# A streaming softmax on one core: row tiles of 3, 5, 15, 15, 25, 25, 10, 15, 15 instead of 3, 5 and eight times 15

## The chip, the core and the metric

The kernel runs on one core of a Trainium2 chip. The metric is device time in microseconds (us); the median of five runs of the kernel before is 159.82 us (159.80 to 167.6, four of the five between 159.80 and 159.89).

## What is computed

A softmax with temperature 2 over the last axis of a 16 x 1024 x 512 array in 32-bit floats. That is 16,384 rows of 512 numbers, 33.55 MB in and as much out.

```
x_scaled = x / 2.0
exp_x = exp(x_scaled - max(x_scaled, axis=-1))
out = exp_x / sum(exp_x, axis=-1)
```

The kernel takes the exponential without subtracting the row's maximum, and checks afterwards that every row sum lies between 1.0 and 1e30. Only if one does not is everything computed again, with the maximum subtracted (the loops inside `rounds`, L142 to L151). For the inputs here that second way is not taken.

## The kernel before, in words

**Layout.** The 16,384 rows are spread over 128 partitions, so that each partition handles 128 rows. In this text a "row" is from here on one such slot: 128 rows of the input, one on each partition, 2048 bytes on each partition. The 128 rows are cut into tiles by the list `TILES` (L10 to L12): pairs of a row count and a place in `arena`, an on-chip buffer with room for 98 rows (L15). A tile of r rows is moved by one DMA in which each partition gets one contiguous run of r x 2048 bytes: 30,720 bytes for 15 rows. With 128 partitions over 16 DMA engines each engine gets 8 such runs of every tile.

**Loads.** Tile 0 is loaded from SP's queue and all other tiles up to the arena's end from ACT's queue, one behind the other, at the very start (`early`, L153; `loads`, L157; `load`, L113). The two last tiles do not fit and are written over tiles 0 to 2 and tile 3, which must have been stored by then. `LATE` (L14) says which stores each of them waits for, and GpSimd (POOL) issues them: it first waits until the rows below `TURN` (L22) have had their exponential (L176), then for the stores (L178), then issues the load (L179).

**Exponential.** When a tile has landed, TensorE's queue, which has hardly any other work, gives ACT one permit for each chunk of the tile (L193, L194); a chunk is 5 rows (3 for the first tile). So a tile's first exponential can start only when all of the tile has landed. ACT takes the exponential of each row in place and its sum along with it (L204, and the loop `exponentials`, L259 to L276).

**Scaling.** DVE takes groups of up to three chunks of one tile (`pairs`, L82 to L88; in the last tile each chunk alone): a reciprocal of the sums (L166), and one multiplication over the whole group (L169).

**Stores.** SP stores the tiles in order, each when all groups of the tile have been scaled (`store`, L135 to L137; `upto`, L89; L211). Load and store of one tile thus have the same run length.

**End.** After the last exponential POOL, DVE and TensorE check the row sums (L180 to L190), and SP waits for all stores.

A tile's order is therefore: load, exponentials, multiplications, store; the four parts of different tiles run beside each other, and what ties them is the arena's room and the order in three DMA queues: q10 in the profile is ACT's (loads), q1 is SP's (tile 0's load and all stores), q0 is POOL's (the two late loads).

Of the kernel before, what the change touches and what calls it, by code (L numbers as in the profile page):

```python
# [7 lines left out]


TILES = [  # L10
    (3, 0), (5, 3), (15, 8), (15, 23), (15, 38), (15, 53), (15, 68), (15, 83), (15, 0), (15, 15),
]  # L12

LATE = {8: (0, 1, 2), 9: (3,)}  # L14
ARENA = 98  # L15

HEAD = [3]
# [1 line left out]

SPREAD = 1  # L20

TURN = 83  # L22

LO, HI = 1.0, 1.0e30
G = 64
# [3 lines left out]
def kernel(  # L29
# [61 lines left out]
    ld = [nc.alloc_semaphore(f"ld{t}") for t in range(len(tiles))]  # L91
    s_home = {t: nc.alloc_semaphore(f"s_home{t}") for t in LATE}
    s_near = nc.alloc_semaphore("s_near")
# [19 lines left out]
    def load(eng, t):  # L113
        r = tiles[t][1]
        parts = [(0, P, 0, r)]
        if t == SPREAD:
            parts = [(0, P, 0, r - 1), (0, 126, r - 1, r), (126, P, r - 1, r)]
        for p, q, lo, hi in parts:
            eng.dma_start(  # L119
                out=sb(t)[p:q, lo:hi], in_=dram(xf, t)[p:q, lo:hi]  # L120
            ).then_inc(ld[t], 16)

    stored_by = {u: s_home[t] for t, us in LATE.items() for u in us}
    for t, (_, r, at) in enumerate(tiles):
        over = {u for u, (_, ru, au) in enumerate(tiles[:t]) if at < au + ru and au < at + r}
        assert over <= {u for v, us in LATE.items() if v <= t for u in us}

    def landings(ts):
        return 16 * len(list(ts))
# [27 lines left out]
    def loads():  # L157
        for t in range(2, min(LATE)):
            load(nc.scalar, t)

    def program():
# [13 lines left out]
        nc.gpsimd.memset(ones[:, :], 1.0).then_inc(s_ones, 1)  # L175
        nc.gpsimd.wait_ge(s_exp, starts.index(TURN))  # L176
        for t, us in LATE.items():
            nc.gpsimd.wait_ge(s_home[t], landings(us))  # L178
# [143 lines left out]
```

## Time and profile before

| | |
|---|---|
| median of 5 runs | 159.82 us |
| the profiled execution's own time | 159.85 us |
| its span, first to last instruction | 158.5 us |
| time outside the span | 1.35 us |
| bytes read / written | 33.55 / 33.55 MB |
| ACT busy | 80.6 us (51%) |
| DVE busy | 73.2 us (46%) |
| stores: issues, KB each for 15 rows | 10, 3840 |

Times in the profile are counted from the first instruction. A packet in the profile's DMA rows is one contiguous run of one partition, or a 4-byte packet that reports an engine's part of a DMA as done. The share of a queue is the time that its packets took, divided by the time of all 16 DMA engines. A DMA's landing is the moment at which all of its parts are reported.

### The profile page before, as it was taken

How to read it: one execution, taken by the hardware profiler on the slowest of the kernel's cores; microseconds unless marked ns; L12 is line 12 of the kernel's file. 1: busy time of each engine (PE TensorE's matmuls, PEld its weight loads, DVE VectorE, ACT ScalarE, POOL GpSimd, SP SyncE). 2: the span in 40 equal slices, each digit the busy share in tenths (PEclk: the TensorE clock that was granted, in tenths of full speed). 3: DMA queues.
4: the chain of work that ended last, by engine and by line, in shares of the span. 5: the costliest groups of instructions: out<-in, count | busy, mean ns of one | idle time of the engine just before them, and what ended most of it. 6: DMA issues, size and time to landing. Idle time of an engine off the chain costs nothing. (4 is left out here: it accounts for less than half of the span.)

```text
span 158.5 us, 657 instructions
## 1 busy us (share of the span) xinstructions
PE 0.2 (0%) x2; PEld 0.1 (0%) x2; DVE 73.2 (46%) x27; ACT 80.6 (51%) x257; POOL 2.2 (1%) x8
## 2 busy tenths in 40 slices
PE   0000000000000000000000000000000000000000
PEld 0000000000000000000000000000000000000000
DVE  0047001992981990059500991008931990993000
ACT  0590598697498008940399001991498008950000
POOL 0000000000000000000000300000000000010000
DMA  7999998999999999999999999999989898989896
GB/s 267 387 496 395 462 408 349 478 390 481 419 442 426 426 442 426 442 419 450 419 450 419 450 403 465 395 473 395 473 380 488 380 488 380 488 372 496 372 481 264
DMA packets 3025, 67.11 MB, mean 423 GB/s; under 512 B 337, under 2 KB 337, under 8 KB 721
## 3 DMA queue, kind: packets, MB, share of 16 engines
q1 hardware_dynamic: 1584, 34.34, 50.6%
q10 hardware_dynamic: 1152, 24.90, 37.0%
q0 software_dynamic: 288, 7.86, 11.6%
q14 instruction: 1, 0.00, 0.0%
HBM read 33.55 MB, written 33.55 MB: 423 GB/s over the span
## 5 line engine op out<-in xcount | busy, mean ns | idle before, releaser
L271 ACT ACTIVATE arena<-arena x125 | 76.6, 614 | 54.3 <-ACTq L140 54.3
L169 DVE TENSOR_TENSOR arena<-arena,recip 128x7680 f32<-128x7680 f32 (+2 forms) x12 | 70.2, 5847 | 0.4
L166 DVE RECIPROCAL recip<-stats 128x15 f32<-128x15 f32 (+2 forms) x12 | 2.7, 224 | 70.5 <-ACT arena L271 61.5
L271 ACT ACTIVATION_READ_ACCUMULATOR arena<-arena x125 | 23.3, 187 | 0.0
L200 ACT ACT_TABLE_LOAD x1 | 1.3, 1283 | 5.8 <-issue 5.8
L119 POOL DMA_DIRECT2D arena<-in_x_dram x2 | 1.3, 636 | 84.9 <-ACT arena L271 84.9
L204 ACT ACTIVATE arena<-arena 128x512 f32<-128x512 f32 x3 | 1.9, 618 | 0.0
L180 POOL TENSOR_SCALAR inside<-stats 128x128 f32<-128x128 f32 x1 | 0.6, 630 | 51.9 <-ACT arena L271 51.9
L204 ACT ACTIVATION_READ_ACCUMULATOR arena<-arena 128x1 f32 x3 | 0.6, 186 | 0.0
L196 PE MATMUL total<-ones,count 128*1 128x1 f32 x2 | 0.2, 164 | 144.1 <-DVE inside L184 144.1
L184 DVE SCALAR_TENSOR_TENSOR inside<-inside,stats 128x128 f32<-128x128 f32 x1 | 0.3, 285 | 0.0
L188 DVE TENSOR_SCALAR flag<-total 1x1 int32<-1x1 f32 x1 | 0.1, 147 | 0.3 <-PE total L196 0.3
L196 PEld LDWEIGHTS total<-ones,count 128*1 128x1 f32 x2 | 0.1, 80 | 144.1 <-DVE inside L184 144.1
L175 POOL MEMSET ones<- 128x1 f32 x1 | 0.1, 98 | 2.2 <-POOLq L37 2.2
L306 POOL MEMSET const-float32-0.0<- 128x1 f32 x1 | 0.1, 104 | 0.2 <-issue 0.2
L306 POOL MEMSET const-bfloat16-1.0<- 128x1 bf16 x1 | 0.1, 107 | 0.0
L306 POOL MEMSET const-uint8-127<- 128x1 uint8 x1 | 0.1, 107 | 0.0
L306 POOL MEMSET const-float32-1.0<- 128x1 f32 x1 | 0.1, 104 | 0.0
L184 DVE DVE_READ_ACCUMULATOR inside<-inside,stats 128x1 f32 x1 | 0.1, 83 | 0.0
## 6 DMA issues: line engine op xcount, KB each, us to landing
out_dram<-arena SPq DMA_DIRECT2D x8, 3840.0 KB, 26.2
arena<-in_x_dram ACTq DMA_DIRECT2D x6, 3840.0 KB, 46.6
arena<-in_x_dram POOLq DMA_DIRECT2D x2, 3840.0 KB, 33.9
out_dram<-arena SPq DMA_DIRECT2D x1, 1280.0 KB, 23.6
arena<-in_x_dram ACTq DMA_DIRECT2D x1, 1024.0 KB
arena<-in_x_dram SPq DMA_DIRECT2D x1, 768.0 KB, 5.6
out_dram<-arena SPq DMA_DIRECT2D x1, 768.0 KB, 15.5
arena<-in_x_dram ACTq DMA_DIRECT2D x1, 252.0 KB
```

What stands on the lines that cost most here:

```text
L119: eng.dma_start(out=sb(t)[p:q, lo:hi], in_=dram(xf, t)[p:q, lo:hi]).then_inc(ld[t], 16)
L166: nc.vector.reciprocal(out=recip[:, b : b + c], in_=stats[:, b : b + c])._wait_ge(s_exp, ks[-1] + 1).then_inc(s_rec, 1)
L169: nc.vector.tensor_mul(out=arena[:, a : a + c], in0=arena[:, a : a + c], in1=recip[:, b : b + c].unsqueeze(2).to_broadcast([P, c, D]),)._w ...
L175: nc.gpsimd.memset(ones[:, :], 1.0).then_inc(s_ones, 1)
L180: nc.gpsimd.tensor_scalar(out=inside[:, :], in0=stats[:, :], scalar1=LO, scalar2=HI, op0=Alu.max, op1=Alu.min,)._wait_ge(s_exp, len(sizes) ...
L184: nc.vector.scalar_tensor_tensor(out=inside[:, :], in0=inside[:, :], scalar=1.0, in1=stats[:, :], op0=Alu.mult, op1=Alu.is_equal, accum_ou ...
L188: nc.vector.tensor_scalar(out=flag[:, :], in0=total[:, :], scalar1=float(N), scalar2=None, op0=Alu.is_ge,)._wait_ge(s_tot, 1).then_inc(s_f ...
L196: nc.tensor.matmul(total[:, :], lhsT=count[:, :], rhs=ones[:, :], start=True, stop=True)._wait_ge(s_cnt, 2).then_inc(s_tot, 1)
L200: nc.scalar.preload_act_table(Exp)
L204: ins = nc.scalar.activation(out=arena[:, b], in_=arena[:, b], func=Exp, scale=0.5, accum_out=stats[:, b : b + 1],)
L271: ins = nc.scalar.activation(out=data, in_=data, func=Exp, scale=0.5, accum_out=stats[:, r : n_rows - E + 1 + r][:, bass.ds(now, 1)],)
L306: nc = _bacc.Bacc("TRN2", target_bir_lowering=False, num_devices=1)
```

## The change

Only three constants change. The 60 rows of tiles 4 to 7 (four tiles of 15) become three tiles of 25, 25 and 10 rows, so there are nine tiles instead of ten. The two late tiles keep their size, their places and the stores that they wait for, and are now numbers 7 and 8. POOL's first wait is for the exponentials of rows 0 to 62 (up to the end of the first 25-row tile) instead of rows 0 to 82.

```
 TILES = [
-    (3, 0), (5, 3), (15, 8), (15, 23), (15, 38), (15, 53), (15, 68), (15, 83), (15, 0), (15, 15),
+    (3, 0), (5, 3), (15, 8), (15, 23), (25, 38), (25, 63), (10, 88), (15, 0), (15, 15),
 ]
 
-LATE = {8: (0, 1, 2), 9: (3,)}
+LATE = {7: (0, 1, 2), 8: (3,)}
...
-TURN = 83
+TURN = 63
```

What follows from it in the code: a run is 51,200 bytes in the 25-row tiles and 20,480 in the 10-row tile. A 25-row tile gets five permits at once when it has landed; DVE scales it in a group of three chunks and a group of two; its store waits for both. ACT still runs 26 chunks; the DVE groups are 13 instead of 12: of 3 and 5 rows, then 15, 15, 15 and 10, 15 and 10, 10, 15, and three times 5.

## Prediction

> **What bounds the kernel now.** I read the page first, for the engines and the DMA row.
>
> ```profile
> span 158.5 us, 657 instructions
> ...
> PE 0.2 (0%) x2; PEld 0.1 (0%) x2; DVE 73.2 (46%) x27; ACT 80.6 (51%) x257; POOL 2.2 (1%) x8
> ...
> DMA  7999998999999999999999999999989898989896
> ...
> DVE 6%; PE 0%; issue 0%; ACT 0%
> ```
>
> No compute engine is busy for much over half of the span, while the DMA row stands at 8 or 9 in every slice but the first and last. The last line is the chain of work that ended last. It covers 6% only: it begins at 134.43 us with an exponential and ends at 144.3 us, because it doesn't follow transfers. What bounds must be looked for in the queues, so I asked for the DMA view of the stretch from 1 to 158 us (queue: packets, MB, share of 16 engines):
>
> ```profile
> DMA packets 3024, 67.11 MB, mean 427 GB/s; under 512 B 336, under 2 KB 336, under 8 KB 720
> ...
> q1 hardware_dynamic: 1584, 34.34, 51.1%
> q10 hardware_dynamic: 1152, 24.90, 37.4%
> q0 software_dynamic: 288, 7.86, 11.7%
> ```
>
> The shares add up to 100.2%: all 16 DMA engines work without a pause from 1 to 158 us (a little over 100%, since packets overlap slightly). The time is the work of the DMA engines plus 1 us ahead and 0.5 us behind. So a change helps only if it makes that work less, and hurts only if it makes it more or leaves the queues empty for a while. Two things are then wanted: what a packet costs by its size, and how near the queues come to running empty.
>
> For the first I took the stretch from 28.8 to 36.5 us, in which q1 moves only 10,240-byte packets (tile 1's store) and q10 only 30,720-byte ones:
>
> ```profile
> DMA packets 161, 3.31 MB, mean 430 GB/s; under 512 B 0, under 2 KB 0, under 8 KB 0
> ...
> q10 hardware_dynamic: 81, 2.49, 74.8%
> q1 hardware_dynamic: 80, 0.82, 25.0%
> ```
>
> A packet of 30,720 bytes takes 0.748 x 7.7 us x 16 / 81 = 1.138 us, one of 10,240 bytes 0.250 x 7.7 x 16 / 80 = 0.385 us. The line through both is 0.0087 us plus 0.03675 us per 1000 bytes. The packet counts show a second thing: 81 against 80. An engine takes one packet from each queue in turn, whatever its size.
>
> For the second I took the stretches at the end (us, then busy time and instructions of PE, PEld, DVE, ACT, POOL, then clock, DMA share, GB/s):
>
> ```profile
> 131.10:143.80 12.70, 0.00 (x0) 0.00 (x0) 9.04 (x7) 9.29 (x30) 0.63 (x1) 1.00 0.99 428
> 143.80:149.40 5.60, 0.19 (x2) 0.09 (x2) 0.35 (x3) 0.00 (x0) 0.00 (x0) 1.00 1.01 433
> 149.40:158.50 9.10, 0.00 (x0) 0.00 (x0) 0.00 (x0) 0.00 (x0) 0.00 (x0) 1.00 0.88 378
> ```
>
> The last load lands at 131.1 us. Until its tile's store is issued, at 143.83 us, ACT and DVE work 9.3 and 9.0 us, and the DMA engines live on the stores before it (0.99). The store before the last lands at 149.4 us; the last needs the 9.1 us after that.
>
> **The change part by part.**
>
> *Packets.* By the line, a 51,200-byte packet costs 1.890 us and a 20,480-byte one 0.761 us. Each engine loses 4 x 8 packets of 15 rows (load and store: 64 x 1.138 = 72.8 us) and gets 2 x 8 x 2 of 25 rows and 8 x 2 of 10 rows (32 x 1.890 + 16 x 0.761 = 72.7 us): the bytes are the same, and 16 packets' constant part goes, 16 x 0.0087 = 0.14 us, with two 4-byte reports of 0.009 us. As packets overlap a little (the 100.2%), the constant is worth between 0 and that: a gain of 0 to 0.16 us. I take 0.1.
>
> The trace has no 51,200-byte packet. From below it costs its bytes alone, 51.2 x 0.03675 = 1.882 us; from above as much as five packets of 10,240 bytes, 5 x 0.385 = 1.925 us. Over 32 packets on each engine that is 0.3 us less to 1.1 us more than 1.890. I take the line, because it comes out of the nearest row, 30,720 bytes.
>
> *Fixed cost of a DMA.* One load and one store fewer are issued. In the stretch from 132.8 to 147 us q1 works alone, finishes one store and begins the next, with a share of 99.8%: between two DMAs that are both queued there is nothing to save, so I price it at 0. The Trainium skill, "DMA: Bandwidth & Descriptors", section "Anatomy of one DMA — SWDGE (gpsimd) path", fits each DMA as about 2.0 us plus its bytes over 436 GB/s; by that, two DMAs fewer would be an estimated 4 us, and the time about 155.8 us. The 99.8% speaks against it: such a fixed part passes beside the next DMA's bytes here.
>
> *Waits.* A tile's exponentials wait for all of it, and its store for all its groups. I rebuilt the schedule from durations in the trace: an exponential 0.612 us per row (15 rows from 59.85 to 69.03), a multiplication 8.16 us for 15 rows, so 5.4 for 10, a reciprocal 0.28 us, a store's first packet 3.8 us after its issue (35.59 to about 39.3), a POOL load's 5.1 us (87.60 to about 92.7).
> - Until tile 3 has landed (28.8 us) nothing differs.
> - Tile 4: 8 turns on each engine of one load packet (1.890) and one store packet. About 6 packets of tile 1's store are left, then tile 2's store (issued at 35.6) gives two: 6 x 2.275 + 2 x 3.03 = 19.7, landing at about 48. Exponentials until 63.7, first group scaled at 66, second at 72. The store comes 24 us after the landing, where it was 18 (59.5 to 77.64). In this time q1 still has the stores of tiles 2 and 3, issued at 35.6 and 47.0.
> - Tile 5: 8 x (1.890 + 1.138) = 24.2, landing at 72; exponentials until 88, its store at 96.
> - POOL: rows below 63 are done at 63.7, and tile 2's store lands at about 67, so the first late load is issued at 67, not 87.6. Behind that instruction waits the second late load, which needs tile 3's store. The checks (L180) come behind both on POOL, and they wait for the last exponential anyway.
> - From 72 on three queues take turns: tile 6's 0.761, the late load's and tile 3's store's 1.138 each. 6 x 3.04 brings tile 3's store to about 90 and the second late load's issue to 91; two more turns, with tile 4's store packets, end both loads at about 98.
> - The last load: 8 x (1.138 + 1.890) = 24.2 from 98, landing at 122 instead of 131.1. The stores of tiles 5, 6 and 7 are issued at about 96, 109 and 120, so q1 has work. The last store is issued 12.7 us after the landing, at about 135 instead of 143.83.
>
> It must have its first packet when the store before it runs out, near 149; 135 + 3.8 leaves some 10 us, where the kernel before has 149 - 143.8 - 3.8, a bit over 1. The added waits (6 us on tile 4's store, a 13th group on DVE) thus stay under the stores queued before them. If that cover were gone, each us of lateness would cost a us. The late loads' earlier start gains nothing: it changes the order of reads and writes, and the engines work at the same rate in both (432 GB/s from 28.8 to 131, 428 to 433 in the stores-only stretch).
>
> *Sum.* Profiled execution: 159.85 - 0.1 = 159.75 us (span 158.4). The median is 0.03 lower than that execution, so 159.7.
>
> **The rivals.** A measurement can tell 0.2% (0.32 us) from no change.
>
> 1. *Slower: the long packets cost more.* Every run of up to 30,720 bytes lies on one line, and nothing in the trace shows a longer one. If the queue cut a 51,200-byte run into single rows, each would cost 0.085 us (72 packets of 2048 bytes in 6.0 to 6.4 us at a share of 96.0%): 25 x 0.085 = 2.13 instead of 1.890, over 32 packets 7.5 us, and the time 167. A milder price, like the 1.925 from above, gives 160.8. It decides from 1.903 us per packet on, 0.7% over the line. For it: no row reaches 51,200. Against it: the straight line. Chance 0.16, mostly of the mild kind.
> 2. *Slower: reads held up, or the queues run empty.* From 12 to 14.9 us, where loads run alone, a 15-row packet takes 0.827 x 2.9 x 16 / 32 = 1.199 us, 5% more. Between 28.8 and about 42 us loads get 83% of the time instead of 75%; half of that 5% on 11 us of load packets is 0.3 us, the whole 0.6: 160.0 to 160.3. A queue that runs empty would need my schedule to be 10 us wrong at the end. Together 0.08.
> 3. *Faster by over 0.3 us.* The bytes-alone price (0.3 us) and the full 0.16, or fewer held reads because long runs of loads alone (38.5 to 39.3 us, when q1 is empty) no longer occur: 159.3. Nothing else is there to win, since the engines have no pause. Chance 0.14.
> 4. *Forecast: within 0.2%*, 159.4 to 160.1: 0.62.
>
> **The numbers.** The likeliest case gives 159.7. The range goes down to 159.3 (rival 3) and up to 160.6, which takes in rival 2 and half of the mild part of rival 1; outside remain the cut packets, the dearest of the mild prices and a gain over 0.5 us, less than 0.2. Faster 0.14, same 0.62, slower 0.16 + 0.08 = 0.24.
>
> **What would show it.** Right: shares of the queues that add up to 100% from 1 us to the end, a 51,200-byte packet of about 1.89 us in a stretch where it is alone on its queue, 2736 packets instead of 3024 (256 fewer, and 32 reports), the last load's landing near 122 and the last store's issue near 135. Wrong: packets of 2048 bytes on q1 after 40 us, a digit under 8 in the DMA row between the first and last slice, or a share below 99%. My forecast fails if the trace shows the engines working as before and the sum of packet times is still over 0.3 us off.

## The result, and the profile after

The changed kernel takes 160.26 us (median of 28 runs, 159.80 to 160.43) against 159.83 us before. The ratio is 1.0024, with a 95% interval of 1.0019 to 1.0029: slower by about 0.4 us. A few executions, whatever the kernel, are disturbed and take 3 to 9 us longer; they are left out of every ratio below and of the medians of e5 and e7, and without them the kernel before lies between 159.76 and 159.97 here. The profiled execution after took 160.28 us, with a span of 159.0 us (before: 159.85 and 158.5).

The page of the kernel after:

```profile
span 159.0 us, 656 instructions
...
DMA  7999998999799989999989899899999999999996
```

The span is 0.5 us longer and one DMA digit inside it reads 7, in slice 11, which is 39.8 to 43.7 us. (A packet counts where it starts, so one 7 alone is not yet a pause.) The DMA view from 1 to 158 us:

```profile
DMA packets 2732, 67.11 MB, mean 427 GB/s; under 512 B 300, under 2 KB 300, under 8 KB 684
...
q1 hardware_dynamic: 1436, 34.34, 51.0%
q10 hardware_dynamic: 1008, 24.90, 37.6%
q0 software_dynamic: 288, 7.86, 11.6%
```

The shares add up to 100.2%, as before: the engines never rest. There are 292 packets fewer (the four reports missing from the forecast 2736 come after 158 us), and yet the packets' time has not become less. q10 shows where: 37.6% for the same bytes in 144 packets fewer, against 37.4%.

The end of the run, in stretches (busy time of PE, PEld, DVE, ACT, POOL; then clock, DMA share, GB/s):

```profile
121.50:135.40 13.90, 0.00 (x0) 0.00 (x0) 13.80 (x8) 9.30 (x30) 1.62 (x1) 1.00 0.97 420
135.40:149.40 14.00, 0.19 (x2) 0.09 (x2) 0.29 (x3) 0.00 (x0) 0.00 (x0) 1.00 1.01 435
149.40:159.00 9.60, 0.00 (x0) 0.00 (x0) 0.00 (x0) 0.00 (x0) 0.00 (x0) 1.00 0.84 362
```

The last load's exponentials begin at 121.85 us and the last store is issued at 135.36. That is 14 us before it is needed, so no queue runs empty here.

**Where the time went.** Tile 1's store ends at about 41.5 us and tile 2's begins. The DMA view from 41.3 to 43.8 us:

```profile
DMA packets 32, 0.94 MB, mean 377 GB/s; under 512 B 12, under 2 KB 12, under 8 KB 12
...
q10 hardware_dynamic: 16, 0.82, 93.3%
q1 hardware_dynamic: 16, 0.12, 11.7%
```

Each engine starts one 51,200-byte load packet in it, and that takes 0.933 x 2.5 x 16 / 16 = 2.33 us. From 39.5 to 43.8 us 32 of them have a share of 100.0%, so 2.15 us each:

```profile
q10 hardware_dynamic: 32, 1.64, 100.0%
```

Elsewhere the same size costs what the line said, here as stores alone from 122 to 133 us, 1.032 x 11 x 16 / 96 = 1.892 us:

```profile
q1 hardware_dynamic: 96, 4.92, 103.2%
```

So the loads are held up there by 2 x 0.26 = 0.52 us on each engine. At the next change, from tile 2's store to tile 3's (62 to 68 us), the same size is not held up, 0.670 x 6 x 16 / 34 = 1.892 us:

```profile
q10 hardware_dynamic: 34, 1.74, 67.0%
```

At the end of tile 1's store in the kernel before (36.5 to 38.5 us) nothing is held up, 0.925 x 2 x 16 / 26 = 1.138 us:

```profile
q10 hardware_dynamic: 26, 0.80, 92.5%
```

**Who pays for it.** Each engine has its fixed 8 of the 128 runs of a tile (only tile 1's load, cut by L117 in all kernels alike, is not shared out evenly), and the kernel ends with the slowest engine. Every engine's last act is a 4-byte report. First the kernel before, from 157.98 us on; then the kernel after, from 158 us on:

```profile
DMA packets 1, 0.00 MB, mean 0 GB/s; under 512 B 1, under 2 KB 1, under 8 KB 1
```

```profile
DMA packets 4, 0.00 MB, mean 0 GB/s; under 512 B 4, under 2 KB 4, under 8 KB 4
```

Before, 15 of 16 engines are done by 157.98. After, 12 are done by 158.0 and four come later, the store's landing being 135.36 + 23.6 = 158.96 us. Most engines have got the 0.52 us nearly back: 0.14 us from the saved packets and 0.2 us from earlier hold-ups that were smaller in this execution (from 24.6 to 27.3 us 32 load packets of 30,720 bytes have a share of 89.3%, before 93.6%, so 2 x 0.06 us; from 12 to 15 us 32 have 76.8% against 79.9%, so 2 x 0.05 us). Four have not.

The packet records tell more. On one engine each packet begins within a few ns of the end of the one before it, so the packets can be followed back from the last report and sorted by engine. "Lost" is then what an engine's packets took over the line's price. Sorted so, every engine loses 0.43 to 0.78 us from 36 to 44.5 us, and none loses anything there before the change. The mean engine's last report comes 0.16 us later than before (157.89 against 157.73 us), the last engine's 0.60 us later (158.58 against 157.98). This last engine loses 0.62 us from 36 to 44.5 us and 0.94 us in all after 20 us, and it was about half a us behind the others already at 20 us. Before the change, too, the engine that ends last was one that was behind at 20 us, but it lost only 0.26 us after that. (One of the other three late ones, at 158.17 us, is late for another reason: it loses 0.45 us after 100 us, in store packets.) So the time follows from a hold-up that all engines meet and that the engine already behind cannot make good.

### The profile page after: what moved, and what is told of

It reads as the page before. It is cut to its first block, busy times and chain, and to the rows that moved or that the text cites. A ratio compares the mean times of both kernels' runs of the same rounds, so it can differ in the third digit from the quotient of the medians.

```text
span 159.0 us, 656 instructions
## 1 busy us (share of the span) xinstructions
PE 0.2 (0%) x2; PEld 0.1 (0%) x2; DVE 73.1 (46%) x29; ACT 80.4 (51%) x257; POOL 3.2 (2%) x8
## 2 busy tenths in 40 slices
DMA packets 2736, 67.11 MB, mean 422 GB/s; under 512 B 304, under 2 KB 304, under 8 KB 688
## 3 DMA queue, kind: packets, MB, share of 16 engines
q1 hardware_dynamic: 1440, 34.34, 50.4%
## 5 line engine op out<-in xcount | busy, mean ns | idle before, releaser
L169 DVE TENSOR_TENSOR arena<-arena,recip 128x7680 f32<-128x7680 f32 (+3 forms) x13 | 70.3, 5409 | 0.4
L166 DVE RECIPROCAL recip<-stats 128x15 f32<-128x15 f32 (+3 forms) x13 | 2.8, 215 | 62.2 <-ACT arena L271 53.6
L180 POOL TENSOR_SCALAR inside<-stats 128x128 f32<-128x128 f32 x1 | 1.6, 1619 | 38.4 <-ACT arena L271 38.4
```

Of the source, the lines that this page charges most:

```text
L166: nc.vector.reciprocal(out=recip[:, b : b + c], in_=stats[:, b : b + c])._wait_ge(s_exp, ks[-1] + 1).then_inc(s_rec, 1)
L169: nc.vector.tensor_mul(out=arena[:, a : a + c], in0=arena[:, a : a + c], in1=recip[:, b : b + c].unsqueeze(2).to_broadcast([P, c, D]),)._w ...
L180: nc.gpsimd.tensor_scalar(out=inside[:, :], in0=stats[:, :], scalar1=LO, scalar2=HI, op0=Alu.max, op1=Alu.min,)._wait_ge(s_exp, len(sizes) ...
```

## The experiments

My first theory (A): loads are held up where they run alone with 51,200-byte packets, at the end of tile 1's store, and the slowest engine keeps the loss. Rival B: the three queues taking turns after the earlier late load. Later ones are named in the expectations: C and F, any change of DMAs beside packets of another size; D, long load packets; E, long store packets; G, the waits for a whole 25-row tile. "Held-up packet" is the mean load packet at the end of tile 1's store, beside its undisturbed price; it is left blank where packets of two sizes meet there. Each kernel was run beside the kernel before, and its ratio is to those runs.

| kernel | median us (range) | ratio to before, 95% interval | held-up packet / price, us |
|---|---|---|---|
| before | 159.83 (159.76 to 159.97) | | 1.138 / 1.138 |
| after | 160.26 (159.80 to 160.43) | 1.0019 to 1.0029 | 2.33 / 1.89 |
| e1_turn_only | 159.88 (159.83 to 160.00) | 0.9994 to 1.0012 | 1.15 / 1.14 |
| e2_tiles_only | 163.22 (162.92 to 164.94) | 1.0196 to 1.0272 | 2.27 / 1.89 |
| e3_ten_first | 161.57 (160.09 to 161.95) | 1.0078 to 1.0128 | |
| e4_split_store | 160.69 (160.21 to 161.11) | 1.0029 to 1.0061 | 2.08 / 1.89 |
| e5_cut_loads | 162.34 (160.34 to 162.47) | 1.0142 to 1.0171 | 1.14 / 1.14 |
| e6_cut_stores | 160.25 (160.03 to 160.47) | 1.0014 to 1.0032 | 2.33 / 1.89 |
| e7_cut_both | 160.29 (160.16 to 162.52) | 1.0018 to 1.0037 | 1.15 / 1.14 |
| e8_tens | 160.62 (160.47 to 161.41) | 1.0036 to 1.0077 | |
| e9_cut_tile4 | 159.85 (159.73 to 160.79) | 0.9999 to 1.0029 | 1.15 / 1.14 |
| e10_twenties | 160.05 (159.75 to 160.50) | 1.0005 to 1.0023 | 1.71 / 1.52 |
| e12_fifteen_first | 160.58 (159.79 to 161.79) | 1.0030 to 1.0079 | 1.14 / 1.14 |
| e13_one_long | 162.38 (162.33 to 162.41) | 1.0140 to 1.0168 | 2.20 / 1.89 |

**e1_turn_only**, on the kernel before:

```
-TURN = 83
+TURN = 63
```

> The kernel before with POOL's first wait alone changed (rows below 63 instead of 83); all tiles stay 3, 5 and eight times 15. Theory A (loads are held up where they run alone with 51,200-byte packets, 41.3 to 43.8 us of the changed kernel, where a load packet takes 0.933 x 2.5 x 16 / 16 = 2.33 us instead of 1.89, and the slowest DMA engine keeps that loss to the end): no long packet, so 159.8 us, as before. Rival B (the three queues taking turns from 72 us on, which the earlier late load brings, spread the engines apart): 160.2 us.

Measured: 159.88 us, no difference. The earlier late load costs nothing beside the old tiles; B falls. Its load packets at the end of tile 1's store take 1.077 x 2 x 16 / 30 = 1.15 us.

**e2_tiles_only**, on the changed kernel:

```
-TURN = 63
+TURN = 88
```

> The changed kernel with POOL's first wait put late (rows below 88, about 88 us, near the 87.6 us of the kernel before). Theory A: the hold-up at 41 us stays, 160.2 us. Rival B: 159.7 us, since the late loads come as late as before.

Measured: 163.22 us, which neither theory said. The hold-up at 41 us is there (0.908 x 2.5 x 16 / 16 = 2.27 us), but most of the loss is at the end. In stretches of this kernel:

```profile
138.50:148.80 10.30, 0.00 (x0) 0.00 (x0) 6.68 (x6) 9.29 (x30) 0.62 (x1) 1.00 0.96 415
148.80:152.20 3.40, 0.19 (x2) 0.09 (x2) 2.72 (x4) 0.00 (x0) 0.01 (x1) 1.00 0.36 154
```

The DMA engines rest for two thirds of 3.4 us. With the late loads issued only at 90.41 and 91.13 us, they run beside tile 4's and 5's stores, whose 51,200-byte packets take 1.89 us of each turn of 1.89 + 1.14. The last load lands at 138.5 us, and the last store is issued at 151.19, when the store before it has run out on most engines at 148.8. The change needs its earlier `TURN`, though that does nothing for the kernel before.

**e3_ten_first**, on the changed kernel:

```
-    ..., (25, 38), (25, 63), (10, 88), ...
+    ..., (10, 38), (25, 48), (25, 73), ...
```

> The changed kernel with the middle tiles in the order 10, 25, 25 instead of 25, 25, 10: the same packets in number and size, but when tile 1's store runs out and tile 2's has not begun, loads run with 20,480-byte packets. Theory A: no long packets alone, no held-up load after 30 us, 159.7 to 159.8 us. Rival C (51,200-byte load packets cost more wherever a store begins or ends beside them): 160.2 us, with load packets of well over 1.89 us at a later change of stores.

**e11_ten_first_again** is the same kernel:

> The kernel of e3_ten_first once more, for a look at an execution near its median of 161.57 us (the trace of e3_ten_first is of its fastest, 160.09 us). If the time is lost by single DMA engines that fall behind: the ends of the last store lie 2 us or more apart over the engines, with their mean near 158 us. If it is lost by a late last store: DMA share under 0.9 somewhere before 150 us.

Measured: 161.57 us. Theory A, which promised 159.8, falls as the whole story: with no long packet at 41 us it is slower still, and it spreads over 1.9 us. The second traced execution took 160.65 us. In its view from 158 to 159.3 us four engines still report, and one of them began a whole packet after 157.2 us:

```profile
DMA packets 4, 0.00 MB, mean 0 GB/s; under 512 B 4, under 2 KB 4, under 8 KB 4
```

From 63 to 70 us its load packets of 51,200 bytes take 0.583 x 7 x 16 / 34 = 1.92 us, so the hold-ups are small on the mean. It is single engines that are behind. An execution near 161.6 us was not seen in a trace, and no spread of 2 us.

**e4_split_store**, on the changed kernel (the waits for tile 1's store count 32 instead of 16):

```
+        for lo, hi in [(0, 3), (3, r)] if t == 1 else [(0, r)]:
             eng.dma_start(
-                out=dram(of, t), in_=sb(t)
+                out=dram(of, t)[:, lo:hi], in_=sb(t)[:, lo:hi]
...
```

> The changed kernel with tile 1's store cut into two DMAs (rows 0 to 2 and rows 3 to 4 of the tile), 16 packets on each engine instead of 8, so that q1 has work from tile 1's store until long after tile 2's store is ready. Theory A: loads are never alone with long packets, no held-up load at 41 us, 159.7 to 159.8 us (the 8 packets more cost at most 0.07 us). Rival C: the hold-up stays at some change of stores, 160.2 us.

Measured: 160.69 us. The hold-up leaves its place: the 51,200-byte packets from 38.9 to 42 us take 0.648 x 3.1 x 16 / 17 = 1.89 us. It comes up where the cut store now ends, from 56 to 58.5 us, with 0.833 x 2.5 x 16 / 16 = 2.08 us:

```profile
q10 hardware_dynamic: 16, 0.82, 83.3%
```

Tile 2's store was issued at 35.93 us, so the store queue was not empty there: loads being alone is not what it takes. Nor does every change of stores do it, since nothing is held up between the two parts; the hold-up goes with the change from tile 1's store to tile 2's. The time does not come back. This trace is of e4's slowest execution, 161.11 us, and has smaller hold-ups besides: from 110 to 120 us the late loads' packets take 0.463 x 10 x 16 / 63 = 1.18 us instead of 1.14.

**e5_cut_loads, e6_cut_stores, e7_cut_both**, on the changed kernel. The first adds these lines to `load` and waits for 32 on those tiles; the second makes the same cut in `store`; the third has both:

```
+        if r == 25:
+            parts = [(0, P, 0, 15), (0, P, 15, 25)]
```

> The changed kernel with the loads of the two 25-row tiles cut into two DMAs, 15 and 10 rows, so that no load packet is over 30,720 bytes; tiles, waits and stores stay. Theory D (51,200-byte load packets are what is held up, unevenly over the engines, and the slowest engine ends the kernel): 159.7 to 159.9 us, the engines' ends within 0.6 us. Rival E (it is the long store packets): 160.2 us. Rival F (packets of different sizes in two queues, of whatever length, put the engines out of step): 160.2 us or more.

> The changed kernel with the stores of the two 25-row tiles cut into two DMAs, 15 and 10 rows, so that no store packet is over 30,720 bytes; loads stay. Theory D: the hold-up at 41 us stays, 160.2 us. Rival E: 159.7 to 159.9 us. Rival F: 160.2 us or more.

> The changed kernel with both loads and stores of the 25-row tiles cut into 15 and 10 rows: its tiles, waits and order, but no packet over 30,720 bytes. Theories D and E: 159.8 to 159.9 us. Rival G (the waits for a whole 25-row tile cost, not the packets): 160.2 us. Rival F: over 160 us, since 10-row and 15-row packets still meet.

Measured: e6, with short store packets, is the changed kernel again, 160.25 us, and its load packets from 40.3 to 43.8 us take 0.666 x 3.5 x 16 / 16 = 2.33 us:

```profile
q10 hardware_dynamic: 16, 0.82, 66.6%
```

E falls: cutting the long store packets changes nothing. In e5 the hold-up is gone (1.068 x 2 x 16 / 30 = 1.14 us), but the kernel takes 162.34 us, because its first late load overtakes tile 6. Tile 6 lands at 114.5 us, its exponentials come first in ACT's order, and the last store is issued at 147.66. In e7 the hold-up is gone too (1.009 x 2.2 x 16 / 31 = 1.15 us). Its traced execution, of 162.52 us, has a DMA share of 0.86 from 139 to 148.6 us, where the stores have run out for a while:

```profile
139.00:148.60 9.60, 0.00 (x0) 0.00 (x0) 9.50 (x8) 1.44 (x6) 2.65 (x1) 1.00 0.86 368
```

That is the longest of e7's executions in the table; the others, 160.16 to 160.85 us, were not traced, and what makes them slower than the kernel before is open. The times of both say nothing on D. Only their hold-up does.

**e8_tens**, on the kernel before:

```
-    ..., (15, 38), (15, 53), (15, 68), (15, 83), (15, 0), (15, 15),
+    ..., (10, 38), (10, 48), (10, 58), (10, 68), (10, 78), (10, 88), (15, 0), (15, 15),
...
-LATE = {8: (0, 1, 2), 9: (3,)}
+LATE = {10: (0, 1, 2), 11: (3,)}
...
-TURN = 83
+TURN = 78
```

> The 60 middle rows as six tiles of 10 rows (20,480-byte packets), POOL's first wait for the rows below 78. Two tiles more than before are 32 packets more on each engine, 0.1 to 0.3 us by the packet line. Theories D and E: 159.9 to 160.1 us with ends within 0.6 us. Rival F: unequal packets meet in the whole middle, so over 160.3 us, and ends over 1 us apart.

Measured: 160.62 us; from 158 us on seven engines still report, where the kernel before has one after 157.98:

```profile
DMA packets 7, 0.00 MB, mean 0 GB/s; under 512 B 7, under 2 KB 7, under 8 KB 7
```

Sorted by engine, the mean of the last reports comes 0.29 us later than before the change (158.02 against 157.73), as much as 32 packets more cost by the line (32 x 0.0087 = 0.28 us), and they lie 0.93 us apart (157.64 to 158.58) where before it is 0.58. No packet here is over 30,720 bytes, so long ones are not needed for a late engine; F's sign, ends over 1 us apart, was just missed. Of the traced execution's 160.65 us 1.65 lie outside the span, 0.3 more than before; that stays unexplained.

**e9_cut_tile4**, on the changed kernel; only tile 4's load is cut (and waited for with 32):

```
+        if t == 4:
+            parts = [(0, P, 0, 15), (0, P, 15, 25)]
```

> The changed kernel with only tile 4's load cut into 15 and 10 rows: at the end of tile 1's store the load packets are then of 30,720 bytes, and tile 5's load keeps its long packets, so that the late loads do not get far ahead of tile 6 and the last store is issued well before 148 us. Theory D (long load packets are held up at the end of tile 1's store): no held-up packet from 36 to 46 us, 159.7 to 159.9 us. If the hold-up merely moves to another change of DMAs: 160.1 us or more, with held-up packets after 46 us.

**e14_cut_tile4_again** is the same kernel:

> The kernel of e9_cut_tile4 once more, for a second look: no held-up load packet from 36 to 46 us again (load packets of 1.14 to 1.15 us at the end of tile 1's store). 159.7 to 159.9 us if no later hold-up comes; where the time is near 160.8 us, as in 2 of its 12 runs, single engines' last packets must lie a us or more behind the others.

Measured: 159.85 us, and 8 of 12 runs at or under 159.90, where the changed kernel has 2 of 28. The profiled execution took 159.73 us. At the end of tile 1's store, from 36.5 to 38.6 us, a load packet takes 1.057 x 2.1 x 16 / 31 = 1.15 us:

```profile
q10 hardware_dynamic: 31, 0.95, 105.7%
```

All its 16 reports come between 157.2 and 158.4 us, one of them after 157.88. With the hold-up gone, the usual time is that of the kernel before; the forecast 159.7 came only in the fastest executions. As e9 still waits for a whole 25-row tile, G falls. Its other runs go up to 160.79, so that its interval reaches as far as the changed kernel's, 1.0029, and the second traced execution took 161.41 us, again without the hold-up (1.093 x 2 x 16 / 30 = 1.17 us). From 158 to 160 us:

```profile
DMA packets 3, 0.03 MB, mean 15 GB/s; under 512 B 2, under 2 KB 2, under 8 KB 2
```

Fourteen engines are done by 158 us, and one begins its last 30,720-byte packet only after it. In this execution the time is lost by one engine falling behind. Sorted by engine, it loses 2.03 us after 20 us and the others 0.12 to 0.95, most of it in load packets that are held up on this engine again and again from 38 to 116 us. The worst begins at 60.48 us; alone in the view from 60.47 to 60.49 us it takes 7.600 x 0.02 x 16 = 2.43 us instead of 1.89:

```profile
q10 hardware_dynamic: 1, 0.05, 760.0%
```

**e10_twenties**, on the changed kernel:

```
-    ..., (25, 38), (25, 63), (10, 88), ...
+    ..., (20, 38), (20, 58), (20, 78), ...
...
-TURN = 63
+TURN = 58
```

> Three tiles of 20 rows (40,960-byte packets) in place of 25, 25 and 10, POOL's first wait for the rows below 58. Theory D: a hold-up from 36 to 46 us between the 0 of 15 rows and the 0.5 us per engine of 25 rows, 159.9 to 160.1 us. Were 51,200 bytes a threshold: no hold-up, 159.7 us.

Measured: 160.05 us. From 36.3 to 40.2 us, 32 load packets take 0.879 x 3.9 x 16 / 32 = 1.71 us; from 29 to 36 us they take 0.786 x 7 x 16 / 58 = 1.52:

```profile
q10 hardware_dynamic: 32, 1.31, 87.9%
```

That is 2 x 0.20 = 0.4 us for each engine, nearly what 25 rows cost. At this place the hold-up sets in between 30,720 and 40,960 bytes. It is no rule for other places: at the end of tile 0's store, from 24.6 to 27.3 us, the kernel before has 30,720-byte load packets of 0.936 x 2.7 x 16 / 32 = 1.26 us instead of 1.14.

**e12_fifteen_first**, on the changed kernel:

```
-    ..., (25, 38), (25, 63), (10, 88), ...
+    ..., (15, 38), (25, 53), (20, 78), ...
...
-TURN = 63
+TURN = 53
```

> Middle tiles of 15, 25 and 20 rows, POOL's first wait for the rows below 53. The load beside the end of tile 1's store has 30,720-byte packets as before the change, and the longer packets come later, beside 30,720-byte stores. Theory D in its narrow form (only that one place): 159.7 to 159.9 us. Theory F (any change of DMAs beside packets of another size can hold loads up): 160.1 us or more, with held-up packets after 46 us.

Measured: 160.58 us, the time that F gave. D in its narrow form falls. But from 52 to 54 us, where no DMA begins or ends, eleven 51,200-byte load packets take 0.700 x 2 x 16 / 11 = 2.04 us, so it does not take the change of DMAs that F names. From 157.3 to 158 us 14 engines report; then, from 158 to 160 us:

```profile
DMA packets 3, 0.03 MB, mean 15 GB/s; under 512 B 2, under 2 KB 2, under 8 KB 2
```

One engine still has a whole 30,720-byte packet to begin. The last store's landing waits for that one engine, over 1 us. Sorted by engine, it loses 2.02 us after 20 us and the others 0.25 to 0.59; three of its 51,200-byte load packets, at 39.57, 45.99 and 52.48 us, take 2.26, 2.34 and 2.47 us. The last of them, alone in the view from 52.47 to 52.49 us (7.731 x 0.02 x 16 = 2.47):

```profile
q10 hardware_dynamic: 1, 0.05, 773.1%
```

**e13_one_long**, on the kernel before:

```
-    ..., (15, 38), (15, 53), (15, 68), (15, 83), (15, 0), (15, 15),
+    ..., (25, 38), (15, 63), (15, 78), (5, 93), (15, 0), (15, 15),
...
-TURN = 83
+TURN = 63
```

> The kernel before with one long tile alone: middle tiles of 25, 15, 15 and 5 rows (ten tiles as before), POOL's first wait for the rows below 63. Only tile 4's load and store have 51,200-byte packets. Theory D: the hold-up at 41 to 44 us comes back whole, load packets there of about 2.3 us, and the time is 160.1 to 160.4 us. If the hold-up needs the rest of the change (tile 5's long packets behind, fewer tiles): load packets of 1.89 us there and 159.8 us.

Measured: the hold-up comes back with the one long load, from 40.9 to 43.3 us, with 0.916 x 2.4 x 16 / 16 = 2.20 us, 0.31 us on each engine where the changed kernel loses 0.52:

```profile
q10 hardware_dynamic: 16, 0.82, 91.6%
```

The time, 162.38 us, is 2 us over the expected 160.1 to 160.4, for another reason. The 5-row tile 7 gets only 0.385 us of a turn and lands at about 120 us; ACT takes tiles in order, so it stands still from 104.0 to 120.48 us though tile 8 landed at about 98. The last stores come late, and the DMA share falls to 0.40:

```profile
139.40:142.40 3.00, 0.00 (x0) 0.00 (x0) 2.97 (x3) 2.62 (x10) 0.29 (x1) 1.00 0.40 171
```

## Why the prediction was wrong

- **What bounds the kernel**: right. The shares sum to 100.2% before and after.
- **The packets' price**: right for an undisturbed one, 1.892 us against 1.890, and no packet was cut. The gain of 0.1 us from the saved packets is not shown as a time: e9's profiled execution took 159.73 us, but its median, 159.85, is that of the kernel before.
- **The fixed cost of a DMA**: right at 0. Two DMAs fewer gave no 4 us, as the 99.8% said against the Trainium skill's formula ("DMA: Bandwidth & Descriptors", section "Anatomy of one DMA — SWDGE (gpsimd) path"), which is fitted to DMAs issued by GpSimd; the two saved here were ACT's and SP's.
- **The schedule**: right where it counts. The last load lands at about 121.5 us (122), the last store is issued at 135.36 (135), the late loads at 67.36 and 92.35 (67 and 91). Tile 5's last report, on the engine that is most behind, came at 75.4 us where I had 72.
- **"The late loads' earlier start gains nothing"**: wrong as a step. e1 confirms it for the old tiles, but with the long ones a start near the old one makes the changed kernel 3.0 us slower (e2, 163.22 against 160.26). I had priced that edit beside the old stores and not beside the new ones. It did not touch the sum, since both edits are made together.
- **"The engines work at the same rate in both"**, and with it the sum: the step that failed. I took the order of reads and writes to be free and an undisturbed price for every packet. The held loads came up as rival 2, but as a matter of the reads' share, with 0.08 together with an empty queue. That the measured 160.26 us lies in its 160.0 to 160.3 is luck: from 28.8 to 39.2 us, where it put the loss, nothing was held up (load packets of 50.4 KB on the mean took 0.773 x 10.4 x 16 / 69 = 1.86 us, the line's price). The loss came at the end of tile 1's store: 0.52 us on each engine that the sum had at 0. e9, e5 and e7 take it away by shorter loads, e4 moves it with the end of the store, e13 puts it into the kernel before with a single long load (0.31 us), and e6 shows that the length of the store packets has no part in it.
- **The sum was made for the mean engine.** The mean engine ends 0.16 us later than before the change, the last one 0.60 us later. e12 and e14 show a time over a us longer from one engine alone. I had no term for this, and the 0.14 us saved are smaller than it.

What is settled: long load packets are held up at that change of stores, and late single engines set the end. What stays open: what in the memory or the DMA engines holds them up, why at that change and not at the next, why there between 30,720 and 40,960 bytes, and why in some executions one engine's loads are held up again and again elsewhere (e12, e14). With these, taking one hold-up away does not make every execution fast. The Trainium skill, "DMA: Bandwidth & Descriptors", section "Latency and other measured facts", gives 0.2 us for an HBM access on average and 2 us at high load; no run here shows whether that is what the packets waited for. No version beat the kernel before beyond its interval.

## What to carry to other kernels

When the DMA engines are busy throughout, do the sum for the slowest engine, not the mean: as long as the queues stay full, nothing evens out what one of them loses, and a gain of a few packets' overhead is smaller than one hold-up. Only an empty queue does even it out: in e2 and e13, where the stores run out ahead of the last one, all 16 last reports come within 0.2 us (from 161.18 and from 160.44 us). Changing one packet size against another changes each queue's part of every turn, so go through who is starved at the end (e2, e5 and e13 lost 2.5 to 3.4 us that way) before looking at the overhead saved. And an edit that costs nothing alone can be what keeps the other one from being slow: try them apart.

## What the runs showed of the hardware

- A DMA engine took one packet from each queue in turn whatever its size (81 against 80 before; sorted by engine, none took two running from one queue from 28.8 to 36.5 us). The Trainium skill, "DMA: Bandwidth & Descriptors", section "Queues, rings and completion order", has an engine drain about 9 to 17 descriptors before it changes queues; here, with one contiguous run to a packet, it is one run.
- A store's first packet came 3.8 us after its issue while other packets were queued, but under 1 us after it where the engines were idle: in e2 issued at 151.19 us, with the first ten packets before 152.1.
- The price of a packet is a straight line up to 51,200 bytes (1.892 us measured, 1.890 from the line), as long as nothing holds the packet up. Held-up load packets of that size took up to 2.5 us (39 to 44.5 us of the changed kernel, and 2.47 us in e12).
